# Reordering vector work in the last product group of a hybrid decoder kernel

## The chip, the cores and the metric

The kernel runs on one core of a Trainium2 chip. The metric is the device time of one execution in microseconds (us). A profile of one execution shows each engine's instructions: PE (TensorE, matmuls), DVE (VectorE), ACT (ScalarE), POOL (GpSimd, which also issues some transfers) and SP (SyncE, which issues most transfers). Each engine takes its instructions in the order written and waits on semaphores for the others.

## What the kernel computes

One decoder layer on 512 rows of 1024 features in float32: a normalisation, a wide input projection, three mixers (dilated attention, pooling, a state-space scan) whose gated outputs are merged, a projection w_o with a residual, a second normalisation, a convolutional feed-forward net with a residual, and a final normalisation. What matters here is cut down below:

```python
x = x + merged @ w_o                                   # 512 x 1024
x = x + conv_ffn(rmsnorm(x, ln2_g), w_up, ..., w_down) # inner width 2816
return rmsnorm(x, final_g)                             # x * rsqrt(mean(x*x) + 1e-6) * g
```

## The kernel before

Every float32 product is made of three matmuls on split operands: a value is a high part (made by a cast on ACT, tile `wh` for weights, line 195) and a low part (value minus high part, made on DVE, tile `wl`, line 217); `mm3` (line 238 issues its matmuls) adds high x high, high x low and low x high.

A list of jobs sets the order of nearly all work. A job is one block of weights. While job n computes, `prepare` makes the low part of job n+1, casts job n+2 and starts the transfer of job n+3. Within a job's body `step()` is called between pieces; it advances every coroutine in the list `running` to its next `yield`, so work put there (`running.append(...)`) is written into the engines' queues at a later `step()`. `after(n, it)` lets n steps go by before `it` starts. The order of the instructions of PE, ACT, DVE and POOL is the order in which the program writes them.

Two groups near the layer's residuals use Strassen-like products: seven products of quarter-size blocks in place of eight, which accumulate into banks of PSUM. These are the group of w_o (`wo_group`) and the group that ends the kernel (`last_group`), the last part of w_down. Both have jobs named two, five, three, one, six, seven, four, in this order. Each job makes two row blocks of 128 rows (i = 0, 1; row block tb = 2*hi + i) in two banks. Products that share a bank pair (`more=True`) add onto what is there, so before a product adds to a bank, the previous result in it must have been read. In the last group two and five each open a pair of banks and three adds to five's; one opens another pair, and six, seven and four add to it, one behind the other. The read is `dve.tensor_tensor(t, t, bank[i], op)` (line 1656; line 1346 in the group of w_o), which adds the bank to the residual tile `X1[tb, h]`, h being the left or right half of the 1024 columns; products two and five are copied by ACT instead and added by a transfer of POOL.

Some weights are sums of blocks. `W[0]`, `W[1]`, `W[2]` are tiles loaded by SP, to which POOL's transfers add other blocks. The weights of four are `four.raw + W[2]`, made in place on DVE by `total` (line 1668).

`behind` is what a job does after each read. `first(tb, h)` starts the final norm of a row block with its first half: the sum of squares on ACT (line 439) and x*g on POOL (line 1606; line 1289 in the group of w_o). `then(tb, h)` goes on when the second half is there: two one-column operations on DVE (tiles va and vo, lines 1612 and 1613; 1298 and 1299 in the group of w_o), then `norm_late` up to its `yield`: the second half's sum of squares and a square root on ACT (lines 439, 464) and the one-column operation `v` on DVE (line 469), which needs that sum of squares. After the `yield` comes the scaling: `r`, `rt`, `rt` (lines 472 to 474), one half of the output on DVE (line 478) and the other on ACT (line 479); then the output transfers (line 1626). The last row block takes lines 468, 482 and 483 in place of 478 and 479. For row blocks 0 and 1, which six completes, the part after the `yield` goes into `running`; for 2 and 3, which four completes, it is written at once. In the group of w_o the same `norm_late` is followed by transposes on PE (`norm_turn`, lines 453, 456, 457), and the scaling of blocks 2 and 3 is put in among the first products of the feed-forward net (line 1536), together with the low part of their weights.

Of the kernel before, what the change touches and what calls it, by code (L numbers as in the profile page):

```python
# [13 lines left out]
OP = mybir.AluOpType  # L14
# [4 lines left out]
D = 1024  # L19
# [63 lines left out]
def trunk(ctx: ExitStack, tc, out, x, rel_bias, ln1_g, w_in, b_gate, w_a, pool_w, pool_scale, w_b,  # L83
# [3 lines left out]
    act, dve, pool, pe, sp = nc.scalar, nc.vector, nc.gpsimd, nc.tensor, nc.sync  # L87
# [18 lines left out]
    def T(name, dt=F32, shape=(P, S)):  # L106
        return big.tile(list(shape), dt, name=name, tag="t")

    def MM(name):
        return psum.tile([P, S], F32, name=name, tag="mm")  # L110
# [4 lines left out]
    def small(name, shape, dt=F32):  # L115
        return tiny.tile(list(shape), dt, name=name, tag="tiny")
# [7 lines left out]
    waiting, running = [], []  # L124
# [30 lines left out]
    def step():  # L155
        flush()
        if waiting:
            running.append(iter(waiting.pop(0)))
        now = [(it, 0) for it in running]
        for phase in (0, ROWS, WHOLE, REST):  # L160
            now = [(it, advance(it, phase) if at == phase else at) for it, at in now]

    def after(n, it):
        for _ in range(n):
            yield
        yield from it
# [269 lines left out]
    def squares(eng, src, ss):  # L436
        junk = T("junk")
        if eng is act:
            act.activation(junk, src, AF.Square, accum_out=ss)
        else:  # L440
            dve.scalar_tensor_tensor(junk, src, 1.0, src, OP.mult, OP.mult, accum_out=ss)

    def grow(src):
        g = [T("grow") for _ in range(2)]
        for h in range(2):
            sp.dma_start(g[h], src[h * S:(h + 1) * S].partition_broadcast(P))
        return g
# [11 lines left out]
    def norm_late(t, g, v0, outs, last, h=1, apart=False):  # L459


        ss, v, sq, r, rt = (small(n, [P, 1]) for n in ("ss", "v", "sq", "r", "rt"))
        squares(act, t, ss)
        act.activation(sq, ss, AF.Sqrt, bias=v0, scale=1.0 / D)
        xg = None
        if not apart:
            xg = T("xg")
            dve.tensor_tensor(xg, t, g[h], OP.mult)
        dve.scalar_tensor_tensor(v, ss, -0.5 / D, last, OP.mult, OP.add)
        yield xg  # L470

        dve.reciprocal(r, sq)
        dve.scalar_tensor_tensor(rt, r, v, r, OP.mult, OP.mult)
        dve.scalar_tensor_tensor(rt, rt, 1.5, r, OP.add, OP.mult)

        if apart:
            o1, (o0, x0) = outs()
            dve.scalar_tensor_tensor(o1, t, rt, g[h], OP.mult, OP.mult)
            act.mul(o0, x0, rt)
            return  # L480
        (o1, x1), (o0, x0) = outs(xg)
        act.mul(o0, x0, rt)
        dve.tensor_scalar(o1, x1, rt, None, OP.mult)
# [1091 lines left out]
    def last_group():  # L1575
        n = (KF - KS) // 2
        quarter = lambda two, h: w_down[KS * P:, h * S:(h + 1) * S].rearrange(
            "(k two p) c -> two p k c", two=2, p=P)[two]
        pairs = range(KS // 2, KF // 2)
        W, A, B = {}, [], []  # L1580

        def side(j):
            if j == "A11":
                return [FS[0, p] for p in pairs]
            if j in ("A12", "A22"):
                half = LO if j == "A12" else HI
                return [[t[:, half] for t in ACTS[2 * p + 1]] for p in pairs]
            return [FS[j, p] for p in pairs]

        def load(i, two):  # L1590
            W[i] = ypool.tile([P, 4, S], F32, name="w3", tag="xs")[:, :n, :]
            sp.dma_start(W[i], quarter(two, 1))

        def plus(i, two, h):
            for k in range(n):
                pool.dma_start(W[i][:, k, :], quarter(two, h)[:, k, :], accum_op=OP.add)

        def begin():
            fin["g"] = grow(final_g)
            act.activation(small("sq", [P, 1]), eps, AF.Sqrt)  # L1600

        def first(tb, h):
            half = 1 - h
            ss, xg = COLS[tb][0], T("xg")
            squares(act, X1[tb, half], ss)
            pool.tensor_tensor(xg, X1[tb, half], fin["g"][half], OP.mult)
            fin[tb] = ss, xg

        def then(tb, h):
            ss, xg0 = fin[tb]  # L1610
            _, v0, vh = COLS[tb]
            dve.tensor_scalar(v0, ss, 1.0 / D, EPS, OP.mult, OP.add)
            dve.tensor_scalar(vh, v0, -0.5, None, OP.mult)
            o = {1 - h: xg0}
            if tb < 3:
                o[h] = T("xg")
                it = norm_late(X1[tb, h], fin["g"], v0, lambda: (o[h], (xg0, xg0)), vh, h, True)
                next(it)
            else:
                it = norm_late(X1[tb, h], fin["g"], v0, lambda xg: ((xg, xg), (xg0, xg0)), vh, h)  # L1620
                o[h] = next(it)

            def rest():
                next(it, None)
                for i in (h, 1 - h):
                    (sp if i == h or tb < 3 else act).dma_start(
                        out[tb * P:(tb + 1) * P, i * S:(i + 1) * S], o[i])
                yield

            if tb < 2:  # L1630
                running.append(rest() if tb else after(1, rest()))
            else:
                for _ in rest():
                    pass

        def job(j, raw, form, bank, outs, more=False, op=OP.add, behind=None, side_add=False):
            hi, h = outs

            def body(ws):
                wh, wl = ws  # L1640
                if not more:
                    bank[:] = [MM("pb") for _ in range(2)]
                parts = side(j)
                for i in range(2):
                    o = slice(i * P, (i + 1) * P)
                    mm3(bank[i], lambda k: wh[:, k, :], lambda k: wl[:, k, :],
                        lambda k: parts[k][0][:, o], lambda k: parts[k][1][:, o], range(n),
                        flip=True, onto=more)
                    tb = 2 * hi + i
                    t = X1[tb, h]  # L1650
                    if side_add:
                        r = T("r7")
                        act.copy(r, bank[i])
                        pool.dma_start(t, r, accum_op=OP.add)
                    else:
                        dve.tensor_tensor(t, t, bank[i], op)
                    if behind:
                        behind(tb, h)
                    step()

            new = Job([raw] if raw is not None else [], n, S, body)
            new.form, new.once = form, True
            if raw is None:
                new.load = lambda: None
            return new

        def total(out, a, b, op=OP.add):
            dve.tensor_tensor(out, a, b, op)
            return out

        def one_read(tb, h):
            if tb == 0:
                total(four.raw, four.raw, W[2])
            first(tb, 1)

        two = job("A12", quarter(1, 0), None, B, (0, 0), side_add=True)
        five = job(1, None, lambda: W[0], B, (1, 1), side_add=True)
        three = job(4, None, lambda: W[1], B, (0, 1), more=True)
        one = job("A11", quarter(0, 0), None, A, (0, 0), behind=one_read)
        six = job(2, None, lambda: W[2], A, (0, 1), more=True, op=OP.subtract, behind=then)  # L1680
        seven = job(3, None, lambda: W[1], A, (1, 1), more=True, op=OP.subtract,
                    behind=lambda tb, h: first(tb, 0))
        four = job("A22", quarter(1, 0), None, A, (1, 0), more=True, behind=then)
        three.then = lambda: plus(1, 0, 1)

        def soon():
            four.load = None
            fetch(four)
            four.load = lambda: None

        six.load = soon
        return load, plus, begin, [two, five, three, one, six, seven, four]
# [111 lines left out]
    first = [MM("pa") for _ in range(4)]  # L1804
# [63 lines left out]
    for tb in range(2):  # L1868
        s0, s1, v, sq, r, rt = (small(n, [P, 1]) for n in ("s0", "s1", "v", "sq", "r", "rt"))
# [25 lines left out]
    ss = row_squares(2, small("ss", [P, 4]), 2)  # L1895
# [105 lines left out]
```

## Time and profile before

| | us |
|---|---|
| median of 3 runs | 1020.98 (1020.85 to 1021.42) |
| the profiled execution | 1020.77 |
| span of that execution, first to last instruction | 1019.0 |
| PE busy in the span | 1004.1 |
| DVE, ACT, POOL busy | 730.4, 528.4, 164.2 |

Rows of a timeline read: start in us, duration in us, engine, line, operation, output tile <- input tiles, shapes, count; in brackets the time the engine stood idle before it and what released it. A wait row reads: the waiting engine, tile and line <- the releasing engine, tile and line: us in total, number of waits, longest. Consecutive DVE instructions overlap by a little under 0.1 us, so the pitch of starts is shorter than the duration.

### The profile page before, as it was taken

To read this page: it belongs to the slowest core of one execution; us is meant where nothing else is said; L and a number is where in the kernel's file an instruction comes from. 1 tells how busy PE (TensorE), PEld (TensorE's weight loads), DVE (VectorE), ACT (ScalarE), POOL (GpSimd) and SP (SyncE) were. 2 spreads that over 40 slices of the span, in tenths; PEclk is the share of its full clock that TensorE was granted. 3 is DMA by queue.
4 is the path that set the end of the run, shared out by engine and by line. 5 is a ranking of instruction groups with operands and counts; after the bars stand their busy time and mean duration, and the time that the engine had idled before them with its cause. 6 is when DMAs were issued, how large, how long until landed. Compare 5 with 4: busy or idle time off the path is not lost.

```text
span 1019.0 us, 13694 instructions
## 1 busy us (share of the span) xinstructions
PE 1004.1 (99%) x5360; PEld 855.0 (84%) x5360; DVE 730.4 (72%) x931; ACT 528.4 (52%) x895; POOL 164.2 (16%) x144
## 2 busy tenths in 40 slices
PE   9999999999999999999999999999999999999995
PEld 8998878999988888888888887898888888888884
DVE  6564768677757647666889688768768768686786
ACT  6433546564435476879466245554444444443554
POOL 1791000010000000000054501301111110122043
PEclk9999999999999999999999999999999999999998
DMA  8548312155253343552256346332322324342572
GB/s 272 168 107 204 101 66 76 57 155 166 92 182 107 91 124 104 145 144 84 83 155 167 124 145 164 129 124 86 122 83 83 124 82 138 100 125 76 180 164 85
DMA packets 117728, 127.03 MB, mean 125 GB/s; under 512 B 6788, under 2 KB 96455, under 8 KB 117664
## 3 DMA queue, kind: packets, MB, share of 16 engines
q1 hardware_dynamic: 111887, 116.39, 36.9%
q0 software_dynamic: 5184, 8.92, 5.3%
q8 instruction: 42, 0.69, 0.3%
q10 hardware_dynamic: 592, 0.86, 0.2%
q14 instruction: 23, 0.18, 0.0%
HBM read 121.30 MB, written 3.00 MB: 122 GB/s over the span
## 4 chain that ended last, share of the span: by engine, by line
PE 94%; DVE 4%; issue 1%; ACT 1%; DMA 1%; ACTq 0%; DVEq 0%
PE pa L238 36%; PE pu L238 22%; PE pb L238 8%; PE pd L238 7%; PE pqk L238 6%; PE pq L238 3%; PE pa L1849 2%; PE ps L775 1%; DVE wl L217 1%; PE ppw L238 1%; PE po L823 1%; PE pt L809 1%; PE py L1108 1%; PE pu L1536 1%; DMA xin<-in_x_dram 1%
## 5 line engine op out<-in xcount | busy, mean ns | idle before, releaser
L217 DVE TENSOR_TENSOR wl<-raw,wh 128x2048 fp32r<-128x2048 f32 (+3 forms) x86 | 200.5, 2332 | 43.9 <-ACT wh L195 33.9
L195 ACT CAST wh<-raw 128x1024 fp32r<-128x1024 f32 (+3 forms) x169 | 169.9, 1022 | 50.6 <-DVE raw L361 17.8
L1433 DVE SCALAR_TENSOR_TENSOR hc<-pu,fcol,hc 128x510 f32<-128x510 f32 x88 | 65.9, 748 | 53.0 <-ACT hc L1430 51.4
L238 PE MATMUL pa<-uh,wh 128*128 128x512 f32 (+1 forms) x368 | 88.8, 381 | 0.0
L238 PE MATMUL pa<-ul,wh 128*128 128x512 f32 (+1 forms) x368 | 86.8, 375 | 0.0
L238 PE MATMUL pa<-uh,wl 128*128 128x512 f32 (+1 forms) x368 | 86.8, 375 | 0.0
L238 PE MATMUL pu<-uh,wh 128*128 128x512 f32 (+1 forms) x352 | 83.6, 379 | 0.0
L238 PE MATMUL pu<-ul,wh 128*128 128x512 f32 (+1 forms) x352 | 83.5, 379 | 0.0
L238 PE MATMUL pu<-uh,wl 128*128 128x512 f32 (+1 forms) x352 | 83.5, 379 | 0.0
L238 PEld LDWEIGHTS pa<-ul,wh 128*128 128x128 f32 x368 | 66.7, 188 | 12.6
L238 PEld LDWEIGHTS pa<-uh,wl 128*128 128x128 f32 x368 | 66.7, 188 | 12.5
L238 PEld LDWEIGHTS pa<-uh,wh 128*128 128x128 f32 x368 | 65.3, 189 | 11.8
L1438 POOL TENSOR_TENSOR hc<-hc 128x512 f32<-128x512 f32 x22 | 29.9, 1361 | 280.1 <-DVE hc L1433 243.3
L238 PEld LDWEIGHTS pu<-ul,wh 128*128 128x128 f32 x352 | 64.2, 188 | 12.5
L238 PEld LDWEIGHTS pu<-uh,wl 128*128 128x128 f32 x352 | 64.2, 188 | 12.5
L238 PEld LDWEIGHTS pu<-uh,wh 128*128 128x128 f32 x352 | 64.1, 188 | 12.4
L1430 ACT ACTIVATE hc<-pu,fcol,fcol 128x512 f32<-128x512 f32 x40 | 31.2, 779 | 75.0 <-PE pu L238 75.0
L217 DVE TENSOR_TENSOR wl<-w,wh 128x2048 fp32r<-128x2048 f32 (+1 forms) x26 | 54.8, 2107 | 10.2 <-issue 4.6
L195 ACT CAST wh<-w 128x1024 fp32r<-128x1024 f32 (+1 forms) x52 | 47.2, 950 | 9.1 <-DMA w<-in_ffn_w_down_dram 4.3
L797 ACT ACTIVATE sb<-sb,nmls 128x128 f32<-128x128 f32 (+1 forms) x72 | 30.0, 418 | 31.4 <-DVE nmls L794 20.8
L1091 POOL TENSOR_TENSOR st<-st,dts 128x512 f32<-128x512 f32 x4 | 4.2, 1051 | 226.0 <-ACT st L1099 163.9
L1435 ACT ACTIVATE hc<-hc 128x512 f32<-128x512 f32 x22 | 13.9, 632 | 40.3 <-DVE hc L1433 40.3
(438 smaller groups left out, 1979.8 us busy)
## 6 DMA issues: line engine op xcount, KB each, us to landing
raw<-in_w_in_dram SPq DMA_DIRECT2D x24, 1024.0 KB, 5.7
raw<-in_ffn_w_up_dram SPq DMA_DIRECT2D x22, 1024.0 KB, 5.3
raw<-in_w_in_dram SPq DMA_DIRECT2D x14, 512.0 KB, 5.5
raw<-in_w_in_dram SPq DMA_DIRECT2D x8, 768.0 KB
raw<-in_ffn_w_down_dram SPq DMA_DIRECT2D x6, 1024.0 KB, 5.0
raw<-in_w_b_dram SPq DMA_DIRECT2D x4, 1024.0 KB
al<-ad SPq DMA_DIRECT2D x16, 256.0 KB, 6.6
raw<-in_w_c_dram SPq DMA_DIRECT2D x4, 1024.0 KB, 5.0
```

Source lines behind the costliest of these rows:

```text
L195: (other.tensor_copy if other and i else act.copy)(job.high[:, :, o], job.raw[:, :, o])
L217: (eng or dve).tensor_tensor(l[:, :, o], job.raw[:, :, o], h[:, :, o].bitcast(F32), OP.subtract)
L238: pe.matmul(ps, l, r, start=first and n == 0, stop=last and n == total - 1, skip_group_check=onto)
L775: pe.matmul(pss[i][:, o:o + w * P], q[r, n * P:(n + 1) * P], k[r, kb * P:(kb + w) * P], start=True, stop=True)
L797: act.activation(sb[:, off:off + w * P], sb[:, off:off + w * P], AF.Exp, bias=nm[:, n, h:h + 1], accum_out=ls[:, n, h:h + 1])
L809: pe.transpose(pt[:, o:o + P], sb[:, o:o + P], eye)
L823: pe.matmul(po[DH * hh:DH * hh + DH, n * P:(n + 1) * P], V[g, kb + i][:, (2 * c + hh) * DH:(2 * c + hh + 1) * DH], probs[2 * c + hh, nb][: ...
L1430: act.activation(t, ps, AF.Identity, bias=ff["c1"][:, ff["b"] + m:ff["b"] + m + 1], scale=fw(2, m))
L1433: dve.scalar_tensor_tensor(t[:, sh:], ps[:, :S - sh], fw(k, m), t[:, sh:], OP.mult, OP.add)
L1435: act.activation(t, t, AF.Silu)
L1438: pool.tensor_tensor(a, a, t, OP.mult)
L1849: pe.matmul(first[2 * n + j][:, lo:hi], a[:, k, j * P:(j + 1) * P], b[:, k, lo:hi], start=a is wh and b is uh and k == 0, stop=a is wl and ...
```

## The change

Three edits. In `norm_late` the operation `v` stands behind the `yield` instead of ahead of it, so it is written together with the scaling. In `last_group`, the scaling of row blocks 0 and 1 is put off by two steps each (before: block 0 by one, block 1 by none). And the sum `four.raw + W[2]` is written after the first read of product three instead of after the first read of product one. The code that follows on the engines: on DVE, the order after six's second read is va and vo of block 1, the low part of four's weights, seven's read of tb 2, the scaling of block 0, seven's read of tb 3, the scaling of block 1, four's first read. Before it was va, vo and v of block 1, the two scalings, the low part of four's weights, seven's two reads, four's first read. On ACT the sums of squares of tb 2 and tb 3 stand ahead of block 0's and block 1's scaling. In the group of w_o, v of blocks 0 and 1 stands ahead of the respective r, and v of block 3 behind the low part of the first feed-forward weights (line 217) instead of ahead of it. POOL's list is the same; in SP's, each of the first two output transfers has the other's place.

```diff
@@ norm_late
             dve.tensor_tensor(xg, t, g[h], OP.mult)
+        yield xg
+
         dve.scalar_tensor_tensor(v, ss, -0.5 / D, last, OP.mult, OP.add)
-        yield xg
-
         dve.reciprocal(r, sq)
@@ last_group, then
             if tb < 2:
-                running.append(rest() if tb else after(1, rest()))
+                running.append(after(2, rest()))
@@ last_group
-        def one_read(tb, h):
+        def three_read(tb, h):
             if tb == 0:
                 total(four.raw, four.raw, W[2])
-            first(tb, 1)
...
-        three = job(4, None, lambda: W[1], B, (0, 1), more=True)
-        one = job("A11", quarter(0, 0), None, A, (0, 0), behind=one_read)
+        three = job(4, None, lambda: W[1], B, (0, 1), more=True, behind=three_read)
+        one = job("A11", quarter(0, 0), None, A, (0, 0), behind=lambda tb, h: first(tb, 1))
```

## The prediction

> **What bounds the kernel now.** I read the page's engine totals first, then the chain that ended last, then the waits of PE alone, and last the timelines round them.
>
> ```profile
> PE 1004.1 (99%) x5360; PEld 855.0 (84%) x5360; DVE 730.4 (72%) x931; ACT 528.4 (52%) x895; POOL 164.2 (16%) x144
> ```
> ```profile
> PE 94%; DVE 4%; issue 1%; ACT 1%; DMA 1%; ACTq 0%; DVEq 0%
> ```
>
> TensorE carries the span. An edit on DVE pays only where PE stands still behind DVE, or behind PE's last matmul. The waits of PE show two such places that the edited code reaches, one in 640:672 (the group of w_o) and one in 970:1019 (the last group):
>
> ```profile
> PE pu L1536 <- DVE wl L217: 1.8, 1, 1.8
> PE uT L453 <- ACT u L479: 0.4, 1, 0.4
> ```
> ```profile
> PE pb L238 <- DVE x L1656: 3.1, 1, 3.1
> ```
>
> In the last group's PE and DVE timelines the long stop is the start of product four: its bank is the one that seven's first result (tb 2) still occupies until L1656 has read it.
>
> ```profile
> 993.97 0.84 PE L238 MATMUL pb<-wh,sah 128*128 128x512 f32 x3
> 994.65 0.84 PE L238 MATMUL pb<-wh,sal 128*128 128x512 f32 x3
> ```
> ```profile
> 1001.72 0.84 PE L238 MATMUL pb<-wl,sbh 128*128 128x512 f32 x3
> 1005.61 0.93 PE L238 MATMUL pb<-wh,fh 128*128 128x512 f32 x3 [3.05 <-DVE x L1656]
> ```
> ```profile
> 1000.42 0.16 DVE L469 SCALAR_TENSOR_TENSOR v<-ss,vo 128x1 f32<-128x1 f32 x1 [0.54 <-ACT junk L439]
> ...
> 1003.12 1.75 DVE L217 TENSOR_TENSOR wl<-raw,wh 128x1536 fp32r<-128x1536 f32 x1
> 1004.78 0.68 DVE L1656 TENSOR_TENSOR x<-x,pb 128x512 f32<-128x512 f32 x1
> ```
> ```profile
> 1008.82 0.69 DVE L1656 TENSOR_TENSOR x<-x,pb 128x512 f32<-128x512 f32 x1 [2.76 <-PE pb L238]
> ...
> 1012.00 0.68 DVE L1656 TENSOR_TENSOR x<-x,pb 128x512 f32<-128x512 f32 x1
> ```
>
> PE finished seven at 1002.56 (1001.72 + 0.84), but the two scalings (1000.42 to 1003.12) and the last weights' low part (to 1004.78) stood ahead of the read on DVE. PE lost 3.05 us. It then ran part of four slowly; the stage table says why:
>
> ```profile
> 1006.75:1010.25 3.50, 3.50 (x10) 2.73 (x9) 0.91 (x3) 0.73 (x3) 1.33 (x2) 0.51 0.00 0
> ```
>
> The granted clock was 0.51 for 3.5 us (the column ahead of the last two; 3.50 behind the stretch is its length), which costs PE 3.5 x 0.49 = 1.7. The end follows from DVE's last read, at 1012.00: the tail behind it takes 1019.0 - 1012.00 = 7.0 us and no edit reaches its operations except v, which there has the same neighbours.
>
> **The change, step 1: v behind the yield, in the group of w_o.** The edit is in norm_late, which that group uses too.
>
> ```profile
> 644.75 0.15 DVE L1299 TENSOR_SCALAR vo<-va 128x1 f32<-128x1 f32 x1
> 645.45 0.16 DVE L469 SCALAR_TENSOR_TENSOR v<-ss,vo 128x1 f32<-128x1 f32 x1 [0.54 <-ACT junk L439]
> ...
> 646.16 0.75 DVE L478 SCALAR_TENSOR_TENSOR u<-x,rt,grow 128x512 f32<-128x512 f32 x1
> 646.83 0.15 DVE L472 RECIPROCAL r<-sq 128x1 f32<-128x1 f32 x1
> ...
> 648.14 2.29 DVE L217 TENSOR_TENSOR wl<-raw,wh 128x2048 fp32r<-128x2048 f32 x1
> ```
> ```profile
> 660.60 0.15 DVE L1299 TENSOR_SCALAR vo<-va 128x1 f32<-128x1 f32 x1
> 661.29 0.16 DVE L469 SCALAR_TENSOR_TENSOR v<-ss,vo 128x1 f32<-128x1 f32 x1 [0.54 <-ACT junk L439]
> 661.36 2.29 DVE L217 TENSOR_TENSOR wl<-raw,wh 128x2048 fp32r<-128x2048 f32 x1
> ```
> ```profile
> 660.92 1.04 PE L453 MATMUL uT<-eye,u 128*128 128x128 f32 x8
> 663.71 2.18 PE L1536 MATMUL pu<-uh,wl 128*128 128x256 f32 x16 [1.75 <-DVE wl L217]
> ```
>
> Block 1's v at 645.45 waits 0.54 us for a sum of squares while block 0's scaling, already computable, is queued behind it. An instruction that nothing holds starts 0.07 us after a small one (661.29 to 661.36). So v of block 0 can start at 644.75 + 0.07 = 644.82, its L478 0.71 us later (645.45 to 646.16) at 645.53, which is 0.63 us earlier. Block 1's v then costs 0.07 in its new place: wl at 648.14 is 0.56 us earlier. From that wl to the vo at 660.60 the chain that ended last runs over DVE and ACT in turn and names PE nowhere, so it all moves by 0.56. For block 3, v now stands behind the wl that PE waits for: wl starts at 660.60 - 0.56 + 0.07 = 660.11 instead of 661.36, so it is 1.25 us earlier. PE waits 1.75 there, so all 1.25 arrives, and what is late next is still this wl: PE's uT also moves by the 0.35 or so that it waited for u, and PE goes on idling about 0.85. From there to the last group PE's list of waits is empty (672:977), so the gain is kept unless weights come late. They are asked for by wl's end, which moves with it. The bounds are 0 (another input of those matmuls is late next) and 1.75 (the whole wait); I take 1.25.
>
> **Step 2: the sum of four's weights moves from product one's read into three's** (last group, before's times from here on).
>
> ```profile
> 990.09 0.69 DVE L1656 TENSOR_TENSOR x<-x,pb 128x512 f32<-128x512 f32 x1 [1.35 <-PE pb L238]
> 990.70 1.75 DVE L217 TENSOR_TENSOR wl<-w,wh 128x1536 fp32r<-128x1536 f32 x1
> 992.37 0.68 DVE L1656 TENSOR_TENSOR x<-x,pb 128x512 f32<-128x512 f32 x1
> 992.96 1.75 DVE L1668 TENSOR_TENSOR raw<-raw,w 128x1536 f32<-128x1536 f32 x1
> 994.63 0.68 DVE L1656 TENSOR_TENSOR x<-x,pb 128x512 f32<-128x512 f32 x1
> 995.23 2.25 DVE L217 TENSOR_TENSOR wl<-w,wh 128x1536 fp32r<-128x1536 f32 x1
> ```
> ```profile
> raw<-in_ffn_w_down_dram SPq DMA_DIRECT2D x3, 768.0 KB, 5.6
> ```
> ```profile
> L182 SPq DMA_DIRECT2D raw<-in_ffn_w_down_dram x2: 378/378/378, 973.0 to 977.9; - x2
> ```
>
> The sum takes 1.67 us of DVE's queue in either place (992.96 to 994.63). Its new place follows three's first read, which left DVE idle from 988.74 (990.09 - 1.35). Queued behind it are three's second read (0.3 later, to 991.0), six's wl (to 992.67) and one's first read (to 993.35). PE must see that last one done before six starts on the same bank at 993.97, so about 0.6 us is left and PE loses nothing. Its inputs: four's raw weights were issued at 977.9, such a transfer lands in 5.6, so at 983.5; the other operand is the one that ACT casts at 986.49, so it has landed by then.
>
> ```profile
> 986.49 1.57 ACT L195 CAST wh<-w 128x768 fp32r<-128x768 f32 x2
> ```
>
> In the old place 1.67 us go: one's second read starts when PE delivers it (993.97 - 0.68 + 0.84 + 0.04 = 994.17, the 0.04 being the usual step from a matmul's end to its read), 0.46 earlier, and so do seven's wl and six's first read. PE gains at most 0.2 ahead of seven; I count nothing, since the tail that follows is DVE's.
>
> **Step 3: the scalings stand behind seven's reads.** v's wait goes here too, so six's second read starts when PE delivers it: seven's six groups of three end at 1002.56 and begin 4.1 earlier, so at about 998.3. With va and vo (0.6, 0.18, 0.07 by the rows above and the pitch of the reads, 994.63 to 995.23) four's wl stands at 999.1 to 1000.8, and the read of tb 2 at 1000.8 instead of 1004.78; PE delivered it at about 1000.5 (1001.72 - 3 x 0.68 + 0.84). So PE, done with seven at 1002.56, starts four at once: the 3.05 us go. Behind that read, block 0's v to L478 and on takes 0.60 + 0.71 + 0.67, so tb 3 is read at 1002.75 and done at 1003.43; PE asks for that bank 2.04 us after starting four, at 1004.6. Block 1's scaling adds the same 1.98, to 1004.73, and PE delivers four's first result at 1002.56 + 2.04 + 0.16 + 0.04 = 1004.8. From that read to the last one DVE and ACT take 1012.00 - 1008.82 = 3.18, so the last read is at 1008.0, against PE's end at 1002.56 + 4.1 = 1006.7 at full clock. PE gains 4.75 (3.05 and 1.7 of slow clock), but the last read gains 4.0: late next is DVE, with the scalings that now stand there.
>
> Against it stands a price that moves in: POOL's L1606 for tb 2 and tb 3 now runs beside the two scalings.
>
> ```profile
> 993.14 5.50 POOL L1606 TENSOR_TENSOR xg<-x,grow 128x512 f32<-128x512 f32 x2 [1.30 <-DVE x L1656]
> 1005.54 2.54 POOL L1606 TENSOR_TENSOR xg<-x,grow 128x512 f32<-128x512 f32 x2 [6.91 <-DVE x L1656]
> ```
>
> Two of these took 5.50 us beside DVE's sums and wl (2.25 instead of 1.75 us), 2.54 with DVE idle. A slowing of L478 by the same 1.29 is 0.22 each, 0.44 for two; reads of banks kept 0.68. The bounds are 0 and 0.44; I take 0.2, since POOL's two spans cover DVE's small operations as much as L478. Step 3 gives 3.8. The Trainium skill (GPSIMD Reference, 1. Specifications) says that GpSimd shares its SBUF interfaces with VectorE, with contention where a DVE instruction has two SBUF inputs: by that rule both L478 pay in full, which makes step 3 worth 3.6, and the rows of wl and of the bank reads agree with it.
>
> SP's output transfers of blocks 0 and 1 trade places with each other and follow their scalings; all of them still start before block 2's, and the last transfer, behind the last read, keeps its place.
>
> **The sum.** The profiled execution took 1020.77 (span 1019.0 and 1.77 around it): 1020.77 - 1.25 - 3.8 = 1015.7. The median 1020.98 is 0.2 above that execution, so 1015.9 would be as good a reading; I give 1015.7.
>
> **Rivals.**
> - Only the last group pays (other work binds PE at 663, or later weights take the 1.25 back): 1020.77 - 3.8 = 1017.0. For: the way from u to that wl crosses PE, ACT and DVE, and each can hold it. Against: PE's wait names wl alone, and all that stands ahead of it moves.
> - Four runs at half clock all the same. For the 3.5 us of before, PE would end at 1006.7 + 1.7 = 1008.4 and the last read would stand at about 1008.5: 1016.0. For the whole of four, 4.1 more: 1010.8, the last read gains 1.2: 1018.3. Against: the clock fell only after PE had stood still for 3.05 us. The Trainium skill (TensorE: Matmul & The Clock Gate, Part 1) has the clock halve after an idle window of about 3.4 us; the gap here is shorter, so by that rule strictly read another cause could remain, though no other stretch shown here has a lowered clock.
> - Slower or level: the moved sum waits for its weights. L1668 starts at 988.74 only if both operands have landed; the old place shows it only for 992.96. Later than about 989.3, each us delays six's start one for one, by up to 3.7, and an idle PE of that length cost 1.7 of clock above. At its worst: -1.25 - 3.8 + 3.7 + 1.7 = +0.35, 1021.1; without step 1's gain 1022.4, slower by 0.16%, and past 0.2% if the clock's 1.7 falls due a second time. It decides from a landing 5.8 us later than 983.5.
> - The reordering does not move PE's start, because four's first matmul waits for a later DVE count than the read: only step 1 remains, 1019.5.
>
> **How the numbers follow.** Forecast 0.69; last group alone 0.13; half clock 0.08; late sum 0.06 (half of it slower by over 0.2%); no move of PE 0.04. The first case alone spans 1015.0 (all of the 1.75 and no contention, 1020.77 - 1.75 - 4.0) to 1016.3 (0.6 short on either step). Holding 8 in 10 and both nearest rivals, the range is 1014.9 to 1017.8, a little beyond 1015.0 and 1017.0 for the spread between executions and a half clock of middling length. A change of 0.2%, 2.04 us, is what can be told from none: faster 0.90, same 0.07, slower 0.03.
>
> **What would show it.** Right: no PE wait on L1656 before four, granted clock 1.00 to PE's end, PE's wait at L1536 near 0.85, wl there 1.25 earlier; a last read near 1007 (1008 less 1.25), 7.0 us before the end, behind DVE and not PE. Wrong: a gap of PE ahead of six with DVE idle at L1668; a last read that PE releases; a clock of 0.5 after 1000; or PE waits between 672 and 977.

## The result and the profile after

The changed kernel takes 1017.37 us (median; 1017.20 to 1018.15) against 1021.20 us (1020.04 to 1023.36) for the kernel before in the same comparison: a ratio of 0.9961, 95% interval 0.9948 to 0.9974. The profiled execution took 1017.69 us with a span of 1015.9 us, 3.1 us shorter in both than the one profiled before. So the kernel is faster, inside the range given, but the 1015.7 us foretold is 1.7 us too low: 5.05 us were forecast, and the two profiled executions show 3.1.

Three points in time divide the span: the first matmuls of product seven in the group of w_o (`pb<-wh,sbh`; ahead of them the edits move only block 0's `v`, behind which DVE stood idle for 0.87 us before), the first of product six in the last group (`pb<-wh,sah`), and DVE's last read of a bank. The rows of PE and DVE that mark them, first of the kernel before (its other two marks, 993.97 and 1012.00, stand in the prediction), then of the changed one:

```profile
643.77 1.07 PE L238 MATMUL pb<-wh,sbh 128*128 128x512 f32 x4
```
```profile
644.18 1.07 PE L238 MATMUL pb<-wh,sbh 128*128 128x512 f32 x4
...
660.77 1.04 PE L453 MATMUL uT<-eye,u 128*128 128x128 f32 x8
662.78 2.17 PE L1536 MATMUL pu<-uh,wl 128*128 128x256 f32 x16 [0.97 <-DVE wl L217]
...
993.04 0.84 PE L238 MATMUL pb<-wh,sah 128*128 128x512 f32 x3
...
1000.52 0.84 PE L238 MATMUL pb<-wl,sbh 128*128 128x512 f32 x3
1001.20 0.84 PE L238 MATMUL pb<-wh,fh 128*128 128x512 f32 x3
```

| | before | changed | difference |
|---|---|---|---|
| start to seven in w_o's group | 643.77 | 644.18 | +0.41 |
| from there to six in the last group | 350.20 | 348.86 | -1.34 |
| from there to the last read | 18.03 | 15.85 | -2.18 |
| from there to the end of the span | 7.0 | 7.0 | 0 |

The 0.41 arose ahead of everything that was edited: it stands already in the rows of DVE at 636 (L1372 at 635.96 before, at 636.37 here). PE's stop at L1536 fell from 1.75 to 0.97 us. Ahead of product four (1001.20) PE no longer stops at all: it starts 0.68 us after the group before it, the usual pitch. (Its second half starts at 1003.55, 0.99 behind the group before it, since the read of tb 3 ends only at 1003.49.) The clock stays full there, as the stage table shows (columns as in the prediction; the granted clock ahead of the last two numbers):

```profile
1000.00:1005.00 5.00, 4.86 (x22) 3.69 (x21) 4.82 (x11) 2.17 (x5) 2.58 (x2) 1.00 0.25 93
```

So PE did what was foretold. What fell short is DVE's way to its last read. Its timeline in the last group, and below it POOL's two products x*g for tb 2 and tb 3:

```profile
987.73 1.75 DVE L1668 TENSOR_TENSOR raw<-raw,w 128x1536 f32<-128x1536 f32 x1
...
999.84 0.68 DVE L1656 TENSOR_TENSOR x<-x,pb 128x512 f32<-128x512 f32 x1
1000.44 0.15 DVE L471 SCALAR_TENSOR_TENSOR v<-ss,vo 128x1 f32<-128x1 f32 x1
1000.51 0.16 DVE L472 RECIPROCAL r<-sq 128x1 f32<-128x1 f32 x1
1000.70 1.21 DVE L473 SCALAR_TENSOR_TENSOR rt<-r,v 128x1 f32<-128x1 f32 x1
1001.95 0.16 DVE L474 SCALAR_TENSOR_TENSOR rt<-rt,r 128x1 f32<-128x1 f32 x1
1002.14 0.75 DVE L478 SCALAR_TENSOR_TENSOR xg<-x,rt,grow 128x512 f32<-128x512 f32 x1
1002.81 0.68 DVE L1656 TENSOR_TENSOR x<-x,pb 128x512 f32<-128x512 f32 x1
...
1003.67 1.21 DVE L473 SCALAR_TENSOR_TENSOR rt<-r,v 128x1 f32<-128x1 f32 x1
...
1008.89 0.68 DVE L1656 TENSOR_TENSOR x<-x,pb 128x512 f32<-128x512 f32 x1
```
```profile
1000.61 1.29 POOL L1606 TENSOR_TENSOR xg<-x,grow 128x512 f32<-128x512 f32 x1 [3.67 <-DVE v L471]
1003.57 1.29 POOL L1606 TENSOR_TENSOR xg<-x,grow 128x512 f32<-128x512 f32 x1 [1.68 <-DVE v L471]
```

L473 works on one column and took 0.22 us before, with POOL idle:

```profile
1000.69 0.22 DVE L473 SCALAR_TENSOR_TENSOR rt<-r,v 128x1 f32<-128x1 f32 x1
```

Here it takes 1.21, twice. Both times it ends at the end of a product on POOL: 1000.70 + 1.21 = 1001.91 against 1000.61 + 1.29 = 1001.90, and 1004.88 against 1004.86. That is 0.99 lost twice, 1.98 us, on the way to the last read.

### The profile page after: what moved, and what is told of

It is laid out like the page before. It is cut to its first block, busy times and chain, and to the rows that moved or that the text cites. A ratio compares the mean times of both kernels' runs of the same rounds, so it can differ in the third digit from the quotient of the medians.

```text
span 1015.9 us, 13689 instructions
## 1 busy us (share of the span) xinstructions
PE 1001.6 (99%) x5360; PEld 853.7 (84%) x5360; DVE 730.7 (72%) x931; ACT 527.8 (52%) x895; POOL 163.1 (16%) x144
## 4 chain that ended last, share of the span: by engine, by line
PE 95%; DVE 3%; DMA 1%; issue 1%; ACT 0%; ACTq 0%; DVEq 0%
PE pa L238 36%; PE pu L238 23%; PE pb L238 9%; PE pd L238 7%; PE pqk L238 6%; PE pq L238 3%; PE pa L1848 2%; PE ps L775 1%; PE ppw L238 1%; PE po L823 1%; DVE wl L217 1%; PE pt L809 1%; PE py L1108 1%; PE pu L1536 1%; DMA xin<-in_x_dram 1%
```

## The experiments

The question of the first four: what holds L473? Theory hold: a VectorE instruction with two inputs in SBUF stands still until GpSimd's running instruction is done. Rivals: the engines only share and slow each other (the prediction's pricing), or L473 waits for one of its values.

### POOL's product taken away

```diff
-            pool.tensor_tensor(xg, X1[tb, half], fin["g"][half], OP.mult)
+            if tb < 2:
+                pool.tensor_tensor(xg, X1[tb, half], fin["g"][half], OP.mult)
+            else:
+                xg = X1[tb, half]
```

> The changed kernel without GpSimd's product x*g for row blocks 2 and 3 (line 1606); ACT scales x itself, so one half of the output of those blocks lacks the factor g. Theory hold: a VectorE instruction with two SBUF inputs stands still until GpSimd's running instruction ends, so the two L473 of blocks 0 and 1 fall from 1.21 to 0.22 us, the last bank read comes 2.0 us earlier and the span is 1013.9. Theory share (the prediction's): both engines only slow each other by about 1.29, so L473 was long for that share alone and the gain is at most 0.44 us. Theory wait: L473 waits for something that has nothing to do with GpSimd (the square root, v); nothing changes.

The time is 1015.72 us, ratio 0.9943 (0.9930 to 0.9957), the span 1013.7. DVE's rows, from the first scaling, and the last read:

```profile
1000.48 0.22 DVE L473 SCALAR_TENSOR_TENSOR rt<-r,v 128x1 f32<-128x1 f32 x1
...
1002.46 0.22 DVE L473 SCALAR_TENSOR_TENSOR rt<-r,v 128x1 f32<-128x1 f32 x1
...
1006.69 0.68 DVE L1659 TENSOR_TENSOR x<-x,pb 128x512 f32<-128x512 f32 x1
```

Six starts at 992.81 there, so the last read stands 13.88 us behind it instead of 15.85: 1.97 of the 1.98 us are back. That rules out both rivals: sharing would give 0.44 at most, a wait for a value nothing. The time of 1015.72 is the median of four executions (1015.44 to 1016.43).

### POOL's product in two halves

```diff
-            pool.tensor_tensor(xg, X1[tb, half], fin["g"][half], OP.mult)
+            for o in (slice(0, S),) if tb < 2 else (LO, HI):
+                pool.tensor_tensor(xg[:, o], X1[tb, half][:, o], fin["g"][half][:, o], OP.mult)
```

> The changed kernel with GpSimd's product of blocks 2 and 3 cut into two instructions of 256 columns each. Hold: L473 is released at the end of the first half, so it lasts some 0.5 to 0.6 us, and the second half then holds L474 or L478 or is itself held; the last read moves by 0 to 0.9 us. Share: L473 stays about as it was (1.21), since the bytes are the same. Wait: no change.

The rows of POOL's product for tb 2 and of DVE's scaling of block 0, which meets it:

```profile
1000.37 1.44 POOL L1607 TENSOR_TENSOR xg<-x,grow 128x256 f32<-128x256 f32 x2 [3.85 <-DVE v L471]
```
```profile
1000.47 0.66 DVE L473 SCALAR_TENSOR_TENSOR rt<-r,v 128x1 f32<-128x1 f32 x1
1001.16 0.67 DVE L474 SCALAR_TENSOR_TENSOR rt<-rt,r 128x1 f32<-128x1 f32 x1
```

The hold goes instruction by instruction: a half takes about 0.73, so the first ends near 1001.10 and L473 at 1001.13; the second ends at 1001.81 and L474, which it holds, at 1001.83. The two together lose 0.95 us where L473 alone lost 0.99, and the last read comes 15.76 us behind six. One execution took 1017.35 us.

### L473 and L474 with one tensor input

```diff
-        dve.scalar_tensor_tensor(rt, r, v, r, OP.mult, OP.mult)
-        dve.scalar_tensor_tensor(rt, rt, 1.5, r, OP.add, OP.mult)
+        dve.tensor_scalar(rt, r, v, r, OP.mult, OP.mult)
+        dve.tensor_scalar(rt, rt, 1.5, r, OP.add, OP.mult)
```

> The changed kernel with L473 and L474 written as tensor_scalar with two pointer scalars, so that they have one tensor input. Hold with two inputs: both take 0.16 to 0.22 and the hold moves to L478, which has two tensor inputs; each scaling is about 0.2 us shorter than in the changed kernel, the last read about 0.4 earlier. Hold of any input: the first of them still takes 1.2. Wait: the first still takes 1.2, since it needs the same values.

```profile
1000.73 1.29 POOL L1606 TENSOR_TENSOR xg<-x,grow 128x512 f32<-128x512 f32 x1 [3.67 <-DVE v L471]
```
```profile
1000.83 0.27 DVE L473 TENSOR_SCALAR rt<-r,v 128x1 f32<-128x1 f32 x1
1001.14 0.21 DVE L474 TENSOR_SCALAR rt<-rt,r 128x1 f32<-128x1 f32 x1
1001.39 1.18 DVE L478 SCALAR_TENSOR_TENSOR xg<-x,rt,grow 128x512 f32<-128x512 f32 x1
```

POOL ran from 1000.73 to 1002.02 here. The two operations with one tensor input pass beside it, in the time that they take in block 2 with POOL idle (0.27 and 0.21); L478, the next one with two, takes the hold, 1.18 instead of 0.75. The last read is 15.06 us behind six, 0.8 us better than in the changed kernel and twice what was expected: L478 ends at 1002.57, 0.55 us behind POOL and not 0.75, so that by POOL's recorded end about 0.2 of its own time was spent while it was held. The new form is itself slower (0.27 and 0.21 against 0.22 and 0.16): in the group of w_o, which runs it too, the way to six takes 349.21 instead of 348.86. One execution took 1017.11 us.

### POOL's product moved off the scalings

```diff
-            pool.tensor_tensor(xg, X1[tb, half], fin["g"][half], OP.mult)
             fin[tb] = ss, xg
+            if tb < 2:
+                pool.tensor_tensor(xg, X1[tb, half], fin["g"][half], OP.mult)
+            elif tb == 2:
+                fin[tb] = ss, X1[1, 1]
...
+            if tb == 2:
+                dve.tensor_tensor(fin[3][1], X1[3, 1], fin["g"][1], OP.mult)
...
+                if tb == 1:
+                    pool.tensor_tensor(X1[1, 1], X1[2, 1], fin["g"][1], OP.mult)
```

The first lines stand in `first`, in place of the product there; the next in `then`, behind the operations va and vo; the last behind block 1's output transfers.

> The changed kernel with all work, but GpSimd's product of block 2 stands behind block 1's scaling (it writes over that block's dead residual tile), and block 3's product is done on VectorE where it waits for the sum of squares of block 2. Hold: L473 is 0.22 twice (2.0 us earlier), the new product on VectorE meets the rest of GpSimd's and gives back up to 0.6; last read 1.2 to 2.0 earlier than in the changed kernel, time about 1015.9. Share: 0.1 to 0.4 earlier. Wait: none, or 0.6 later for the added product.

```profile
1003.59 1.29 POOL L1634 TENSOR_TENSOR x<-x,grow 128x512 f32<-128x512 f32 x1 [7.25 <-ACT xg L479]
```
```profile
1004.22 1.21 DVE L1619 TENSOR_TENSOR xg<-x,grow 128x512 f32<-128x512 f32 x1
```

Both L473 take 0.22 again. The new product on DVE meets the end of POOL's and is held for 0.53 (1.21 us, where a product of this size on DVE, L468, takes 0.68). The last read comes 14.11 us behind six, 1.74 better than in the changed kernel. The time is 1015.72 us, ratio 0.9942 (0.9929 to 0.9956): the fastest kernel here that does all the work, and the time that had been foretold for the change itself.

The next four undo or isolate the edits.

### v moved in the group of w_o alone

```diff
-    def norm_late(t, g, v0, outs, last, h=1, apart=False):
+    def norm_late(t, g, v0, outs, last, h=1, apart=False, early=False):
...
+        if early:
+            dve.scalar_tensor_tensor(v, ss, -0.5 / D, last, OP.mult, OP.add)
         yield xg
...
-        dve.scalar_tensor_tensor(v, ss, -0.5 / D, last, OP.mult, OP.add)
+        if not early:
+            dve.scalar_tensor_tensor(v, ss, -0.5 / D, last, OP.mult, OP.add)
...
-                it = norm_late(X1[tb, h], fin["g"], v0, lambda: (o[h], (xg0, xg0)), vh, h, True)
+                it = norm_late(X1[tb, h], fin["g"], v0, lambda: (o[h], (xg0, xg0)), vh, h, True, True)
...
-                it = norm_late(X1[tb, h], fin["g"], v0, lambda xg: ((xg, xg), (xg0, xg0)), vh, h)
+                it = norm_late(X1[tb, h], fin["g"], v0, lambda xg: ((xg, xg), (xg0, xg0)), vh, h, False, True)
...
-                running.append(after(2, rest()))
+                running.append(rest() if tb else after(1, rest()))
```

The calls are those of the last group. The sum is back behind product one too, by the lines shown below for the run on the sum.

> The kernel before with v moved behind the yield in the group of w_o alone; the last group is as before. Theory (the prediction's step 1): PE's wait at L1536 for the low part falls from 1.75 to about 0.95 and, from that transpose to product six, nothing is given back: 1.25 to 1.35 us faster, about 0.13%. Rival: later weights take it back, 0 to 0.3 us.

Ratio 0.9984 (0.9975 to 0.9993), median 1019.80. From seven to six it takes 348.86 us, as in the changed kernel: the 1.34 us are step 1's and are kept. Behind six this execution lost time of its own, below.

### The last group's edits alone

```diff
-                           lambda: (us[h], (us[1 - h], xg0)), vh, h, True)
+                           lambda: (us[h], (us[1 - h], xg0)), vh, h, True, True)
```

The call is that of the group of w_o, with norm_late as in the run before; v is ahead of the yield again there, and the rest is as changed.

> The changed kernel with v ahead of the yield in the group of w_o. Theory: the mid of the kernel is as before (PE waits 1.75 at L1536), and the last read stands 15.85 us behind the start of six against 18.03 before, so 2.2 us faster than before and 1.3 slower than the changed kernel. Rival: the two places are not independent, and the sum of this and the run with w_o alone is not the whole 3.5.

Ratio 0.9987 (0.9978 to 0.9996), median 1019.13. Six to the last read takes 15.84, as in the changed kernel, so by the rows the two places are independent. (The medians of this run and of the one before it lie 2.0 and 1.3 us under that of the kernel before, together 3.3 and not the changed kernel's 3.8; with executions spread over 2.4 and 2.6 us, this decides nothing.) But from seven to six this execution took 351.68, 1.5 us more than the kernel before with the same order there. PE's row and the stage table show where:

```profile
663.96 2.54 PE L1539 MATMUL pu<-uh,wl 128*128 128x256 f32 x16 [1.74 <-DVE wl L217]
```
```profile
664.00:700.00 36.00, 36.00 (x232) 33.52 (x233) 22.71 (x28) 16.63 (x24) 2.59 (x2) 0.95 0.36 118
```

The clock fell behind the stop of 1.74 us. A mean of 0.95 over 36 us is 36 x 0.05 = 1.8 us of PE's work, about the 1.5 that are missing (in this kernel's line numbers the product is L1539).

### The sum back in product one

```diff
-        def three_read(tb, h):
+        def one_read(tb, h):
             if tb == 0:
                 total(four.raw, four.raw, W[2])
+            first(tb, 1)
...
-        three = job(4, None, lambda: W[1], B, (0, 1), more=True, behind=three_read)
-        one = job("A11", quarter(0, 0), None, A, (0, 0), behind=lambda tb, h: first(tb, 1))
+        three = job(4, None, lambda: W[1], B, (0, 1), more=True)
+        one = job("A11", quarter(0, 0), None, A, (0, 0), behind=one_read)
```

> The changed kernel with the sum of four's weights back behind product one's first read. Theory: worth nothing or up to 0.2; one's second read and seven's low part are about 0.5 later and six's second read still starts when PE delivers, so the last read stays 15.8 to 16.1 us behind the start of six. Rival: the sum, two SBUF inputs, now runs beside GpSimd's first product and is held with it, which delays six's reads and makes PE wait 0.5 to 1 ahead of seven.

1017.28 us, ratio 0.9965 (0.9952 to 0.9979); six to the last read 15.85 as with the move. PE loses 0.17 us ahead of seven again, and DVE's way to the end swallows it. The sum was not held by POOL: it started first, at 991.68 against 991.85, and took its usual 1.75.

### v ahead of the yield in the last group

```diff
-                it = norm_late(X1[tb, h], fin["g"], v0, lambda: (o[h], (xg0, xg0)), vh, h, True)
+                it = norm_late(X1[tb, h], fin["g"], v0, lambda: (o[h], (xg0, xg0)), vh, h, True, True)
```

With norm_late as in the run with w_o alone, v stands ahead of the yield in the last group alone, for block 3 as well; all else is as changed.

> The changed kernel with v ahead of the yield in the last group alone; the group of w_o is as changed. Theory: six's second read waits 0.7 behind block 0's v, block 1's v delays four's low part and the read of tb 2 by another 0.6, so all behind it is 1.2 to 1.4 later, less 0.07 for each v taken from the scalings; PE waits up to 0.6 ahead of four, the last read is 1.1 to 1.3 later than in the changed kernel. Rival: the scalings are bound by GpSimd's hold and not by DVE's order, so the delay is swallowed and the change is 0 to 0.3.

1018.20 us, ratio 0.9976 (0.9967 to 0.9986); six to the last read 16.55, 0.70 later. The direction was right and the size too large: block 0's v cost nothing, because its wait was over as six's second result came (DVE waited 0.18 more for PE), and only block 1's wait delayed what follows. PE's stop had the size that was expected, but came ahead of four's second half and not of four itself:

```profile
997.13 0.69 DVE L1659 TENSOR_TENSOR x<-x,pb 128x512 f32<-128x512 f32 x1 [0.18 <-PE pb L238]
```
```profile
1004.06 0.98 PE L238 MATMUL pb<-wh,fh 128*128 128x512 f32 x3 [0.59 <-DVE x L1659]
```

Two of its nine executions took 1019.4 us; no profile shows why.

### The kernel before, profiled three times more

The run with w_o alone and the run of the last group alone each lost time to the clock behind a stop of PE that the kernel before has too. So its own executions should differ.

> The kernel before, looked at again. Theory clock: PE's stop of 1.75 us at L1536 and its stop of 3.05 ahead of four each let the granted clock fall to 0.5 in some executions and not in others, by where the stop falls; the stretch 664:700 shows 1.00 or about 0.95, and the one after 1002 differs in length; the span is near 1018.2 without any fall and near 1020 with two, a mean clock of 0.998 or 0.994. Rival: the spread of the kernel before has another source, and the stretches show the same clock in all looks.

> As the look before it: under theory clock the span follows the two stretches of granted clock (664:700 and behind 1002), under the rival it does not.

> As the two looks before it: under theory clock the span follows the two stretches of granted clock (664:700 and behind 1002), under the rival it does not.

All three show 350.18 to 350.20 us from seven to six and a full clock in 664:700. From six to the last read they take 17.87, 17.95 and 19.05. The stage from 1002 to 1012.5, of the kernel as profiled before and of the third of these:

```profile
1002.00:1012.50 10.50, 6.50 (x21) 4.61 (x19) 6.76 (x15) 3.80 (x9) 2.54 (x2) 0.84 0.27 100
```
```profile
1002.00:1012.50 10.50, 7.46 (x22) 5.66 (x21) 5.79 (x14) 3.38 (x9) 2.51 (x2) 0.67 0.27 100
```

A mean clock of 0.84 over 10.5 us is 10.5 x 0.16 / 0.5 = 3.4 us at half clock; 0.67 is 6.9, twice as long. In the third the clock was at half already while PE still stood (0.52 in 1005:1006; PE starts four at 1005.99), so that about 1 us of the 6.9 cost nothing. The last read comes 1.02 us later for the rest (19.05 against 18.03). The run with w_o alone has 0.67 as well and 19.04. So theory clock holds in part. At the end the clock fell in all four profiles, and its length decides: the spans are 1019.0, 1019.0 and 1019.3 with 0.84, 1020.4 with 0.67. An execution without a fall there was not profiled. For the stop at 662, a fall was seen in the run of the last group alone and in none of the four profiles of the kernel before; how often it happens there is open. The executions of the kernel before spread over 1019.95 to 1021.92 beside the run of the last group alone, those of the changed kernel over 1017.20 to 1018.15; how much of that spread is the clock is not shown.

## Why the prediction was right or wrong

- **What bounds the kernel.** Right: the two stops of PE behind DVE were the places, and one of them vanished and the other shrank to 0.97 (0.85 foretold).
- **Step 1.** It was foretold at 1.25 and measured at 1.34. Every other kernel with this edit shows the same (348.86 to 348.88, against 350.18 to 350.20 without it and without a fall of the clock there), but for the one that also recast L473 and L474 (349.21). The rival that later weights take it back falls.
- **Step 2.** Foretold as worth nothing; it is (15.85 with and without). L1668 started at once behind three's read (987.73), so the rival of the late sum falls.
- **Step 3, PE's part.** Right: no stop ahead of four, full clock. (The 4.1 for six groups is loose: 5 x 0.68 + 0.84 is 4.24, which gives the 998.3 that stands there, and PE's end 0.1 later. Nothing hangs on it.) The rivals "half clock all the same" and "PE's start does not move" fall.
- **Step 3, DVE's part: here the prediction failed.** Without a price for POOL it gave 4.0 us for the last read; the run without POOL's product gives 18.03 - 13.88 = 4.15. The term that was mis-sized is that price: 0.2, with bounds 0 and 0.44, on the thought that both engines slow each other by 1.29 and that L478 pays by its length. Measured: 1.98, on L473, which is a column wide, so the last read gained 4.15 - 1.97 = 2.18 and not 3.8. What counts is not how long DVE's instruction is but how long POOL's still runs. The upper bound was drawn from a ratio of durations, and a ratio can't bound a hold.
- **It could have been read in the profile before.** L1668 ran from 992.96 to 994.71 there and POOL's first product is shown from 993.14; behind a hold it would run 1.29 from 994.71, to 996.0. Then wl, issued at 995.23, would be held to 996.0, run its 1.75 less the 0.2 that L478 above spent while held, and end about 997.55 (it ended at 997.48), and POOL's second would run from there 1.3 us and end at 998.8 (it ended at 998.64). The same pair in the changed kernel, with DVE first:

```profile
994.02 1.76 DVE L217 TENSOR_TENSOR wl<-w,wh 128x1536 fp32r<-128x1536 f32 x1
```
```profile
994.07 2.86 POOL L1606 TENSOR_TENSOR xg<-x,grow 128x512 f32<-128x512 f32 x1 [0.35 <-DVE x L1656]
```

  DVE, first by 0.05, takes its usual 1.76, and POOL 2.86 instead of 1.29. In these pairs whoever came first paid nothing.
- **The rule that was cited.** The prediction took from the Trainium skill (GPSIMD Engine Reference, 1. Specifications) only that the two contend and gave it a ratio as size. The Trainium skill (SBUF — State Buffer, SBUF: two separate sides) is more exact: "The shared pair is an **exclusive lock**, not a bandwidth split"; between a VectorE instruction with two SBUF inputs and a GpSimd one that reads SBUF, whichever starts first keeps the pair for its whole instruction, and the other is blocked. The runs agree: 1.21 with two inputs, 0.27 with one, the hold by instruction when POOL's was cut in two, and 1.76 for the one that came first; only that about 0.2 us of an operation's own time passes while it is held (L473 ends 0.01 behind POOL, L478 0.55) does not fit a full block, unless POOL's recorded ends are late by that much, which no run here shows. With the 0.99 measured for each hold, step 3 is worth 4.0 - 1.98 = 2.0 and the sum is 1017.5, against the measured 1017.37.
- **The sum.** 1020.77 - 1.34 - 2.18 + 0.41 = 1017.7, the profiled execution's 1017.69. Between medians the gain is 3.83 and not 3.1, since the profiled execution of before was one of the shorter ones, and its start was 0.41 shorter; that part was not foretold. The range held because it reached to the rivals, not because its bounds took in the true cost; that was luck. The time lies nearest to the rival in which only the last group pays (1017.0), and that rival's mechanism is false: step 1 paid in full.

## What to carry to other kernels

When work is moved on VectorE, lay it against GpSimd's instructions in time: any VectorE operation with two SBUF inputs, even one column wide, can wait for the end of a GpSimd operation that got there first, so the price here was GpSimd's remaining time. Take a row that is longer than it ought to be and check whether its end coincides with another engine's end; if so a hold is likely, and the run without the other engine's instruction shows it; a ratio of durations then says nothing about the next place. And a stop of TensorE costs more than its length where the clock falls behind it, which a single execution may not show.

## What the runs showed of the hardware that had not been expected

- The hold itself: 0.99 us on an operation that takes 0.22 alone, ended within 0.02 us of GpSimd's end, four times in two profiles (1001.91 and 1004.88 against 1001.90 and 1004.86 in the changed kernel, 1004.58 and 1007.54 against 1004.56 and 1007.52 in the run of the last group alone).
- The granted clock fell to half behind a stop of 1.74 us and behind, or in the last us of, stops of 3.02 to 3.05 us, for 3.4 or 6.9 us, and not always: stops of 1.75 to 1.77 us at the same place left it full in all four profiles of the kernel before. The stops of 0.96 to 1.10 us at L1536, in the kernels that have step 1, were followed by a full clock in every profile here. The Trainium skill (TensorE: Matmul & The Clock Gate, Part 1) has a free-running window of about 3.4 us; the lengths, one and two of these, agree with it, while the stops that sufficed were shorter than the one idle window that the page names.
